# Memory scores in a turn of their own, and V's transposes in another bank, in a hybrid attention layer

## The chip, the cores and the metric

The kernel runs on one core of one Trainium2 chip. The metric is the device time of one execution in microseconds (us); lower is better. The profile is one execution of the same program, taken by the hardware profiler: its engines are PE (TensorE matmuls), PEld (TensorE weight loads), DVE (VectorE), ACT (ScalarE), POOL (GpSimd) and SP (the queue that issues most transfers).

## The reference

One layer of a decoder trunk over 4096 prompt tokens (and 64 sample tokens with caches), width 1024. What matters here is the attention of the prompt:

```python
h = _rmsnorm(x, g_pre); z = h @ w_in
cb, cc, ch, cg, q, k, v, ag, mq, mg = _split_cols(z)
out_a = silu(cg) * cb * conv3(cc * ch)
# window: 8 query heads, 2 kv heads, head_dim 64, blocks of 128 queries
s = q @ k * 0.125 ; s = where(mask, s, -inf)        # 128 own and 128 previous keys
m = maximum(max(s), sink) ; p = exp(s - m)
p = p / (sum(p) + exp(sink - m)) ; o_b = p @ v
# memory: 4 heads, 256 memory tokens
p = softmax(mq @ mk * 0.125) ; o_c = p @ mv
y = concat([out_a, silu(ag) * o_b, silu(mg) * o_c]) @ w_out
x = x + _rmsnorm(y, g_post)
```

## The kernel before, in words

The first part of the program, up to about 931 us, is the input projection (line 368) with its splits and sums; it writes queries, keys, values and gated parts to DRAM. The change does not touch it. The second part interleaves two kinds of work.

**The output projection.** It runs over 33 blocks (`Block.run`, line 1587): 32 of 128 prompt tokens and one of 64 sample tokens. A block's result has two halves of 512 columns (`p`), and each half sums over 8 row tiles (`k`). For one `k` TensorE does three 128x512 matmuls (line 1602), since each operand is split into a high and a low part (`mh`, `ml`, and `wo`). These three matmuls are here called an eighth: a block has 16 eighths.

**The attention.** It runs over half chunks `h = 2c + i` of 128 queries: chunk `c` has 256 tokens, `i` is its half. The half chunks 0 and 1 are done in the first part. The work of each later half chunk is hung into the stream of eighths at places counted from the start of block 0:

- `first_half(h)` at eighth `first_at[h]`: the transposes of the memory probabilities of half `h-1` (tile `xt`, line 1352), the window scores of `h` (`ws`, line 1318), the products of probabilities and values of `h-1` (`wo`, lines 1376, 1382 and 1057), and then, off TensorE, the window softmax of `h` (`sm`) and the gating of `h-1` (lines 1240 and 1393). Where a chunk begins (`i == 0`), V of the chunk is also transposed here (tile `vtp` or `wo`, line 1654), and ScalarE scales the result into `vt` (line 1664).
- `second_half(h)` at eighth `second_at[h]`: the memory scores of `h` (`xs`, line 1340), and right behind them the transposes of the window probabilities (`wt`, line 1364).

Between them the other engines work. For the memory scores: maxima on VectorE (`xmx`, line 1155, and `xnm`), exponentials on ScalarE (`xp`, line 1164), reciprocals on VectorE (`xrd`, line 1170), and the multiplication of `xp` by them on GpSimd (line 1176); only then can `xt` transpose `xp`. For the window: ScalarE copies `wt` to `wpt` (line 1292), GpSimd makes the two masked copies (`wpv`, line 1297, and `wpt`, line 1300), and these go into the products. GpSimd also issues the loads of keys and queries (`kst`, line 1086, and `q`, line 1099). For a block of the projection: `yn` (DVE, line 1609), squares (ACT, line 1610), `yst`, and the split of the next block's input into `mh` (ACT, line 1583) and `ml` (DVE, line 1584).

**PSUM.** All eight banks are given out: two double banks `w` (window scores, window transposes), one double bank `x` (memory scores, memory transposes, products), and two single banks `z` (the projection). The one `x` bank goes round `xt`, `wo`, `xs`: a tile in it can be written once the one before has been read, which for `wo` means the gating, and in a chunk's first half before the change also the scaling of V, which lay in an unused corner of that bank.

**What sets the order.** TensorE's order is the order in which the code is written, up to block 26; after that, and on the other engines throughout, a scheduler puts the instructions in an order when the program is built, and each engine then works strictly in its order.

From half 8 on, `first_at` is one block (16 eighths) after the other, and `second_at` lies 8 eighths behind `first_at`. The halves 2 to 7 are packed more closely by a table of places.

Of the kernel before, what the change touches and what calls it, by code (L numbers as in the profile page):

```python
# [15 lines left out]
P = 128  # L16
# [10 lines left out]
CT = 256  # L27
NCH = 4096 // CT
# [24 lines left out]
def hybrid_layer(ctx: ExitStack, tc: tile.TileContext, a: dict):  # L53
    nc = tc.nc
    TE, V, S, G, DMA = nc.tensor, nc.vector, nc.scalar, nc.gpsimd, nc.sync
# [7 lines left out]
    ident = const.tile([P, P], F32, name="ident")  # L63
# [939 lines left out]
    chunks = {}  # L1003
# [37 lines left out]
    def two_banks(tag, name):  # L1041
        return ps[tag].tile([P, 2, 512], F32, tag=tag, name=name)
# [352 lines left out]
    def chunk_load(c):  # L1395
        if c < NCH:
            chunks[c] = Chunk(c)

            chunks[c].load_queries() if c == 2 else chunks[c].load_keys()
            chunks[c].load_keys() if c == 2 else chunks[c].load_queries()  # L1400
# [238 lines left out]
    def first_half(h):  # L1639

        c, i = divmod(h, 2)
        before = (chunks[(h - 1) // 2], (h - 1) % 2) if 2 < h <= 2 * NCH else None
        if before:
            before[0].memory_transposes(before[1])
        if c < NCH:
            chunks[c].window_scores(i)
        banks = before[0].products(before[1]) if before else None
        new_v = c < NCH and i == 0
        if new_v:
            chunks[c].values(chunks[c - 1].vts[2])  # L1650
            banks = two_banks("x", f"vtp{c}") if banks is None else banks
            t = [banks[:, 1, CT + n * P : CT + n * P + P] for n in range(2)]
            for n in range(2):
                TE.transpose(t[n], chunks[c].vT[:, n * P : n * P + P], ident)
        soon = first_at[h] > 16 * (h - 3) + 4
        if before and soon:
            before[0].gates(before[1], banks)
        if c < NCH:
            chunks[c].window_probabilities(i)
        if before and not soon:  # L1660
            before[0].gates(before[1], banks)
        if new_v:
            for n in range(2):
                S.mul(chunks[c].vts[1 + n], t[n], 0.5)
            chunk_load(c + 1)
        elif c + 1 < NCH:
            chunks[c + 1].load_mix()

    def second_half(h):

        c, i = divmod(h, 2)
        if c < NCH:
            chunks[c].memory_scores(i)
            chunks[c].window_turns(i)


    first_at = {2: 4, 3: 21, 4: 35, 5: 47, 6: 59, 7: 71} | {h: 16 * (h - 3) + 4 for h in range(8, 2 * NCH + 1)}
    second_at = {2: 14, 3: 27, 4: 40, 5: 52, 6: 64, 7: 76} | {h: first_at[h] + 8 for h in range(8, 2 * NCH + 1)}

    def starts_of(i):  # L1680

        at = [(n, lambda h=h: first_half(h)) for h, n in first_at.items()] + [(n, lambda h=h: second_half(h)) for h, n in second_at.items()]
        if i + 1 < len(blocks) and blocks[i + 1].b != 32:
            at.append((max(16 * i, first_at.get(i + 2, 0) + 2), blocks[i + 1].split))
        return {(p, k): lambda now=now: [fn() for fn in now] for p in range(2) for k in range(8)
                if (now := [fn for n, fn in at if n == 16 * i + 8 * p + k])}
# [26 lines left out]
    for i in range(31):  # L1713
        if i == 26:
            turn.close()
        starts = starts_of(i)
        for step in ((p, k) for p in range(2) for k in (1, 3)) if i >= 26 else ():
            starts[step] = lambda before=starts.get(step, lambda: None): (before(), late())
        run(i, starts)
    for stage in stages:  # L1720
        for _ in stage:
            pass
    run(31, starts_of(31))
    run(32, {})
    finish_block()
# [106 lines left out]
```

## Time and profile before

| what | us |
|---|---|
| median of 3 runs | 1549.06 (1541.38 to 1551.43) |
| the profiled execution | 1542.05 |
| its span (first to last instruction) | 1540.3 |
| PE busy in the span | 1520.7 |
| DVE, ACT, POOL busy | 1137.5, 791.0, 393.2 |
| second part (from the first matmul of line 1602) | 931 to 1540 |

Durations and waits below are of the profiled execution. A matmul's duration in the trace is longer than the distance to the next matmul's start, because matmuls are pipelined: what a group costs TensorE is read from its start to the start of the next group.

### The profile page before, as it was taken

What the parts mean: (1) busy time and instruction counts of PE and PEld (TensorE: products, weight loads), DVE (VectorE), ACT (ScalarE), POOL (GpSimd) and SP (SyncE); (2) the same over time, 40 slices, a digit from 0 to 9 for tenths busy, and PEclk for the clock granted to TensorE, in tenths of its full rate; (3) what the DMA queues carried; (4) which work ended last, traced back from release to release, by engine and by line L of the source; (5) the groups of instructions that cost most, each with busy time, mean ns of one, the idle gap of its engine ahead of it and who ended that gap; (6) DMA issues with size and microseconds to landing.
All of it is one profiled execution on the core that took longest, in us unless ns stands there. A gap on an engine that the chain in (4) does not pass through costs nothing.

```text
span 1540.3 us, 30416 instructions
## 1 busy us (share of the span) xinstructions
PE 1520.7 (99%) x11581; PEld 1397.0 (91%) x11581; DVE 1137.5 (74%) x1965; ACT 791.0 (51%) x1949; POOL 393.2 (26%) x635
## 2 busy tenths in 40 slices
PE   9999999999999999999999999999999999999998
PEld 9999999999999999999999998778888888888776
DVE  6789887899988777897677678666666666666653
ACT  6686665476222222445454456555555555555541
POOL 0223232211400000000101203554444444445410
PEclk9999999999999999999999999999999999999999
DMA  9999999878755333678876889967777666666332
GB/s 258 177 240 232 278 284 263 276 241 292 193 180 180 126 126 126 236 223 281 244 269 204 238 295 272 208 140 155 156 155 161 149 149 160 148 148 150 124 123 96
DMA packets 178453, 306.29 MB, mean 199 GB/s; under 512 B 34437, under 2 KB 108165, under 8 KB 178277
## 3 DMA queue, kind: packets, MB, share of 16 engines
q1 hardware_dynamic: 130901, 227.38, 48.2%
q0 software_dynamic: 46688, 75.93, 23.5%
q8 instruction: 91, 1.49, 0.4%
q10 hardware_dynamic: 720, 1.05, 0.2%
q14 instruction: 53, 0.43, 0.1%
HBM read 197.23 MB, written 108.05 MB: 198 GB/s over the span
## 4 chain that ended last, share of the span: by engine, by line
PE 76%; DMA 7%; DVE 5%; POOL 5%; ACT 4%; issue 3%; ACTq 0%; SPq 0%; DVEq 0%; POOLq 0%
PE c L368 47%; PE y L1602 15%; DMA nat<-in_x_p 3%; PE ws L1318 3%; POOL xp L1176 3%; PE wo L1382 2%; PE wo L1057 2%; PE xs L1340 1%; PE wt L1364 1%; PE xt L1352 1%; DMA md<-th 1%; PE wo L1376 1%; POOL wpt L1300 1%; ACT xp L1164 1%; DMA x_0B<-in_xt 1%
## 5 line engine op out<-in xcount | busy, mean ns | idle before, releaser
L1602 PE MATMUL y<-wo,mh 128*128 128x512 f32 (+1 forms) x1040 | 336.1, 394 | 0.0
L375 DVE TENSOR_TENSOR z<-c,z 128x520 f32<-128x520 f32 (+1 forms) x308 | 194.8, 646 | 82.2 <-PE c L368 80.3
L1602 PEld LDWEIGHTS y<-wo,mh 128*128 128x128 f32 x1040 | 194.3, 188 | 42.3 <-issue 4.4
L1602 PE MATMUL y<-wo,ml 128*128 128x512 f32 (+1 forms) x520 | 201.4, 387 | 0.0
L1274 ACT ACTIVATE sm<-sm,wnm 128x128 f32<-128x128 f32 x256 | 99.4, 390 | 70.4 <-DVE wnm L1268 70.4
L1602 PEld LDWEIGHTS y<-wo,ml 128*128 128x128 f32 x520 | 98.0, 188 | 17.7
L1099 POOL DMA_DIRECT2D q<-qd x96 | 59.8, 631 | 139.2 <-PE wt L1364 81.6
L1176 POOL TENSOR_SCALAR xp<-xp,xrd 128x256 f32<-128x256 f32 x128 | 84.9, 675 | 34.8 <-DVE xrd L1170 34.7
L1297 POOL TENSOR_SCALAR_AFFINE_SELECT wpv<-wpt 128x512 f32<-128x512 f32 x62 | 40.4, 665 | 145.4 <-ACT wpt L1292 145.3
L1328 DVE COPY_PREDICATED sm<-wmask,ws 128x512 f32<-128x512 uint8 x60 | 40.6, 732 | 38.2 <-ACT sm L1327 38.2
L737 POOL CAST wmask<-negs 128x256 uint8<-128x256 f32 x1 | 0.9, 930 | 265.8 <-DMA negs<-in_wmask 265.8
L1292 ACT COPY wpt<-wt 128x512 f32<-128x512 f32 x64 | 34.6, 589 | 64.2 <-PE wt L1364 64.2
L1164 ACT ACTIVATE xp<-xs,xnm 128x256 f32<-128x256 f32 x128 | 59.4, 488 | 9.0 <-DVE xnm L1156 6.7
L1155 DVE TENSOR_REDUCE xmx<-xs 128x2 f32<-128x512 f32 x64 | 41.5, 686 | 29.9 <-PE xs L1340 29.8
L1356 ACT COPY xpt<-xt 128x512 f32<-128x512 f32 x30 | 17.6, 586 | 87.3 <-DVE xpt L1356 87.3
L1609 DVE TENSOR_TENSOR yn<-y,gpost 128x512 f32<-128x512 f32 (+1 forms) x66 | 45.1, 683 | 22.1 <-PE y L1602 22.0
L1318 PE MATMUL ws<-kst,q 128*128 128x256 f32 (+1 forms) x480 | 55.8, 298 | 0.0
L276 ACT ACTIVATE nat<-nat 104x1024 f32<-104x1024 f32 x40 | 42.3, 1058 | 26.1 <-DMA nat<-in_x_p 26.1
L1610 ACT ACTIVATE y<-y 128x512 f32<-128x512 f32 (+1 forms) x66 | 39.3, 595 | 30.2 <-DVE yn L1609 30.2
L1300 POOL TENSOR_SCALAR_AFFINE_SELECT wpt<-wpt 128x512 f32<-128x512 f32 x64 | 42.1, 669 | 43.3 <-ACT wpt L1292 43.1
L1356 DVE COPY xpt<-xt 128x512 f32<-128x512 f32 x30 | 20.8, 692 | 42.5 <-PE xt L1352 42.4
L1086 POOL DMA_DIRECT2D kst<-qd x64 | 38.8, 625 | 51.5 <-issue 24.8
(976 smaller groups left out, 5135.5 us busy)
## 6 DMA issues: line engine op xcount, KB each, us to landing
q<-qd POOLq DMA_DIRECT2D x96, 256.0 KB, 4.7
xr<-in_x_p SPq DMA_DIRECT2D x32, 512.0 KB
nat<-in_x_p SPq DMA_DIRECT2D x39, 416.0 KB
o_yp<-xr SPq DMA_DIRECT2D x31, 512.0 KB
md<-th POOLq DMA_DIRECT2D x48, 260.0 KB, 6.6
qd<-zh SPq DMA_DIRECT2D x48, 260.0 KB
qd<-z SPq DMA_DIRECT2D x48, 260.0 KB
kst<-qd POOLq DMA_DIRECT2D x60, 192.0 KB, 4.6
```

Of the source, the lines that this page charges most:

```text
L276: S.activation(t[:RG], t[:RG], AF.Square, accum_out=r[:RG, i : i + 1])
L368: TE.matmul(bank[:, :HW], l, r, start=first and i == 0, stop=last and i == 3 * KH - 1)
L375: add = lambda dst, other: V.tensor_tensor(dst, c, other, op=ALU.add)
L1099: G.dma_start(self.q[64 * half : 64 * half + 64, i : i + 4, :].rearrange("p (j v) n -> p j v n", v=2), heads(part, j, self.ts))
L1155: V.tensor_reduce(mx[:, :nb], s, axis=AX.X, op=ALU.max)
L1164: S.activation(p[:, i, :], s[:, i, :], AF.Exp, bias=nm[:, i : i + 1], scale=SCALE, accum_out=den[:, i : i + 1])
L1176: G.tensor_scalar(p[:, i, :], p[:, i, :], self.rds[h][:, i : i + 1], 0.5, op0=ALU.mult, op1=ALU.mult)
L1274: S.activation(sm[:, hh, :], sm[:, hh, :], AF.Exp, bias=nm[:, hh : hh + 1], scale=SCALE, accum_out=den[:, hh : hh + 1])
L1300: G.affine_select(p3, p3, pattern=[[0, 4], [1, P]], compare_op=ALU.is_ge, fill=0.0, base=0, channel_multiplier=-1)
L1318: TE.matmul(out(kvh, col, bank), q(kvh, col, bank)[r], k(kvh, part)[r], start=first, stop=True, skip_group_check=not first, **place)
L1602: TE.matmul(acc, self.hl[l][:, k], wo[k][c0 // 512][:, r, c0 % 512 : c0 % 512 + c1 - c0], start=j == 0, stop=j == passes * KT - 1)
L1609: V.tensor_tensor(yn[:m, c0:c1], acc[:m], gpost[:m, c0:c1], op=ALU.mult)
```

## The change

The memory scores leave `second_half` and get a turn of their own, `memory_half`, with places `memory_at`. From half 8 on this turn lies 6 eighths behind `first_at`, so two eighths ahead of the window transposes, which stay 8 eighths behind. V's transposes, and the scaling, move from `first_half` into `second_half`, behind the window transposes, and into a double bank `w` in place of the corner of the `x` bank. The table of places for halves 2 to 7 is changed.

```diff
     def first_half(h):
...
         banks = before[0].products(before[1]) if before else None
-        new_v = c < NCH and i == 0
-        if new_v:
-            chunks[c].values(chunks[c - 1].vts[2])
-            banks = two_banks("x", f"vtp{c}") if banks is None else banks
-            t = [banks[:, 1, CT + n * P : CT + n * P + P] for n in range(2)]
-            for n in range(2):
-                TE.transpose(t[n], chunks[c].vT[:, n * P : n * P + P], ident)
...
-        if new_v:
-            for n in range(2):
-                S.mul(chunks[c].vts[1 + n], t[n], 0.5)
+        if c < NCH and i == 0:
             chunk_load(c + 1)
...
-    def second_half(h):
+    def memory_half(h):
         c, i = divmod(h, 2)
         if c < NCH:
             chunks[c].memory_scores(i)
+    def second_half(h):
+        c, i = divmod(h, 2)
+        if c < NCH:
+            if i == 0:
+                chunks[c].values(chunks[c - 1].vts[2])
             chunks[c].window_turns(i)
+            if i == 0:
+                t = two_banks("w", f"vtp{c}")[:, 0].rearrange("p (a n) -> p a n", a=4)
+                for n in range(2):
+                    TE.transpose(t[:, n], chunks[c].vT[:, n * P : n * P + P], ident)
+                for n in range(2):
+                    S.mul(chunks[c].vts[1 + n], t[:, n], 0.5)
...
-    first_at = {2: 4, 3: 21, 4: 35, 5: 47, 6: 59, 7: 71} | {h: 16 * (h - 3) + 4 for h in range(8, 2 * NCH + 1)}
-    second_at = {2: 14, 3: 27, 4: 40, 5: 52, 6: 64, 7: 76} | {h: first_at[h] + 8 for h in range(8, 2 * NCH + 1)}
+    first_at = {2: 4, 3: 19, 4: 33, 5: 46, 6: 59, 7: 71} | {h: 16 * (h - 3) + 4 for h in range(8, 2 * NCH + 1)}
+    memory_at = {2: 11, 3: 24, 4: 38, 5: 51, 6: 64, 7: 76} | {h: first_at[h] + 6 for h in range(8, 2 * NCH + 1)}
+    second_at = {2: 14, 3: 27, 4: 41, 5: 54, 6: 67, 7: 79} | {h: first_at[h] + 8 for h in range(8, 2 * NCH + 1)}
```

On PE, in a chunk's first half in the middle of the second part, the memory scores and the window transposes stand in one turn before the change (`y_1` is the second half of a projection block, `xs_0` the memory scores, `wt` the window transposes; the last number of a name tells tiles of one name apart):

```order
L1602 MATMUL y_1_15509<-wo_1_11845,mh_15162 128x512
L1340 MATMUL xs_0_15522<-mk,q_15055 128x256 x8
L1364 MATMUL wt_15555<-ident,sm_0_15437 128x128 x4
L1364 MATMUL wt_15555<-ident,sm_1_15438 128x128 x4
L1602 MATMUL y_1_15509<-wo_1_11848,mh_15162 128x512
```

At the same place with the change:

```order
L1602 MATMUL y_1_15510<-wo_1_11826,mh_15169 128x512
L1340 MATMUL xs_0_15517<-mk,q_15055 128x256 x8
L1602 MATMUL y_1_15510<-wo_1_11842,mh_15169 128x512
L1602 MATMUL y_1_15510<-wo_1_11842,ml_15170 128x512
...
L1602 MATMUL y_1_15510<-wo_1_11845,mh_15169 128x512
L1364 MATMUL wt_15558<-ident,sm_0_15440 128x128 x4
L1364 MATMUL wt_15558<-ident,sm_1_15441 128x128 x4
L1676 MATMUL vtp_15577<-ident,vT_15053 128x128 x2
L1602 MATMUL y_1_15510<-wo_1_11848,mh_15169 128x512
```

The scores now come six projection matmuls earlier, and V's two transposes (`vtp`) stand behind the window transposes; before, they stood behind the products of the first half.

On POOL, in the same half chunk before the change (`wpv` and `wpt` are the masked copies, `xp` the memory probabilities, `yst` a projection block's norm factor, `kst` the next keys' load):

```order
L1297 AFFINE_SELECT wpv_0_15566<-wpt_0_15564 128x512
L1297 AFFINE_SELECT wpv_1_15571<-wpt_1_15569 128x512
L1300 AFFINE_SELECT wpt_0_15564<-wpt_0_15564 128x512
L1300 AFFINE_SELECT wpt_1_15569<-wpt_1_15569 128x512
L1176 TENSOR_SCALAR xp_0_15539<-xp_0_15539,xrd_0_15547 128x256 x2
L1176 TENSOR_SCALAR xp_1_15543<-xp_1_15543,xrd_1_15551 128x256 x2
L1616 TENSOR_TENSOR yst_15367<-yst_15367,mhalf 128x1
L1086 DMA kst_15915<-qd 64x2x384 x4
```

With the change:

```order
L1176 TENSOR_SCALAR xp_0_15534<-xp_0_15534,xrd_0_15542 128x256 x2
L1176 TENSOR_SCALAR xp_1_15538<-xp_1_15538,xrd_1_15546 128x256 x2
L1297 AFFINE_SELECT wpv_0_15569<-wpt_0_15567 128x512
L1297 AFFINE_SELECT wpv_1_15574<-wpt_1_15572 128x512
L1300 AFFINE_SELECT wpt_0_15567<-wpt_0_15567 128x512
L1300 AFFINE_SELECT wpt_1_15572<-wpt_1_15572 128x512
L1616 TENSOR_TENSOR yst_15374<-yst_15374,mhalf 128x1
L1086 DMA kst_15917<-qd 64x2x384 x4
```

The four multiplications of `xp` have moved from behind the masked copies to ahead of them. In a chunk's second half POOL also issues four loads of `kst` and some of `q` ahead of this; there the two issues of `q` that stood among the masked copies now stand together ahead of `xp`.

On ACT, the same half chunk before the change, behind the last exponential of the window softmax:

```order
L1664 ACTIVATE vt_0_15433<-wo_1_15416 128x128
L1664 ACTIVATE vt_1_15434<-wo_1_15416 128x128
L1610 ACTIVATE y_0_15368,yst_15367<-y_0_15368 128x512
L1292 COPY wpt_0_15564<-wt_15555 128x512
L1292 COPY wpt_1_15569<-wt_15555 128x512
L1164 ACTIVATE xp_0_15539,xden_0_15540<-xs_0_15522,xnm_0_15532 128x256 x2
L1164 ACTIVATE xp_1_15543,xden_1_15544<-xs_0_15522,xnm_1_15536 128x256 x2
L1583 COPY mh_15595<-mix_14834 128x1024
```

With the change:

```order
L1610 ACTIVATE y_0_15375,yst_15374<-y_0_15375 128x512
L1164 ACTIVATE xp_0_15534,xden_0_15535<-xs_0_15517,xnm_0_15527 128x256 x2
L1164 ACTIVATE xp_1_15538,xden_1_15539<-xs_0_15517,xnm_1_15531 128x256 x2
L1292 COPY wpt_0_15567<-wt_15558 128x512
L1292 COPY wpt_1_15572<-wt_15558 128x512
L1678 ACTIVATE vt_0_15556<-vtp_15577 128x128
L1678 ACTIVATE vt_1_15557<-vtp_15577 128x128
L1583 COPY mh_15603<-mix_14840 128x1024
```

The exponentials `xp` have moved ahead of the copies of `wt`, and the two scalings of V from the head of this stretch to behind those copies.

3 lines of the change are left out of this document (2 added, 1 removed).

## The prediction

> **What bounds the kernel now.** I read the page first: the busy times and the chain.
>
> ```profile
> PE 1520.7 (99%) x11581; PEld 1397.0 (91%) x11581; DVE 1137.5 (74%) x1965; ACT 791.0 (51%) x1949; POOL 393.2 (26%) x635
> ...
> PE 76%; DMA 7%; DVE 5%; POOL 5%; ACT 4%; issue 3%; ACTq 0%; SPq 0%; DVEq 0%; POOLq 0%
> ```
>
> TensorE is busy almost throughout, so nothing is gained by making another engine faster; only time in which TensorE waits can be won. A busy TensorE hides short waits, though: a late weight load shows in the next step of a group. So the second view is the waits of the weight loads.
>
> ```profile
> PEld xt L1352 <- POOL xp L1176: 15.8, 45, 1.2
> PEld xs L1340 <- ACT vt L1664: 1.9, 2, 0.9
> ```
>
> The one large wait: the memory transposes `xt` wait for GpSimd's multiplication of `xp`. The other row is the `x` bank held by V's scaling, twice. How much of the 15.8 us costs time is read from the timeline of TensorE, from start to start. First the steady part (a chunk's second half, then the next one's first):
>
> ```profile
> 1102.23 1.11 PE L1340 MATMUL xs<-mk,q 128*128 128x256 f32 x8
> 1103.18 1.04 PE L1364 MATMUL wt<-ident,sm 128*128 128x128 f32 x8
> 1103.98 0.47 PE L1602 MATMUL y<-wo,mh 128*128 128x512 f32 x1
> 1104.29 0.40 PE L1602 MATMUL y<-wo,ml 128*128 128x512 f32 x1
> 1104.53 0.62 PE L1602 MATMUL y<-wo,mh 128*128 128x512 f32 x2
> ...
> 1109.55 1.65 PE L1352 MATMUL xt<-ident,xp 128*128 128x128 f32 x8
> 1110.95 1.86 PE L1318 MATMUL ws<-kst,q 128*128 128x256 f32 x16
> 1112.74 0.43 PE L1376 MATMUL wo<-wpv,vt 64*64 64x256 f32 x2
> ...
> 1115.22 0.44 PE L1654 MATMUL wo<-ident,vT 128*128 128x128 f32 x2
> 1115.42 0.48 PE L1602 MATMUL y<-wo,mh 128*128 128x512 f32 x1
> ...
> 1120.98 1.11 PE L1340 MATMUL xs<-mk,q 128*128 128x256 f32 x8
> ...
> 1128.26 1.29 PE L1352 MATMUL xt<-ident,xp 128*128 128x128 f32 x8
> 1129.31 1.86 PE L1318 MATMUL ws<-kst,q 128*128 128x256 f32 x16
> ```
>
> Eight transposes without a wait take 0.80 us (`wt`: 1103.18 to 1103.98). `xt` takes 1.40 here (1109.55 to 1110.95) and 1.05 in the next half (1128.26 to 1129.31): 0.60 and 0.25 us of waiting, in turn. Reading the 30 groups of `xt` like this, less 0.80 each, gives 13.3 us. The first and the last do not wait, and the largest wait lies in the closely packed halves:
>
> ```profile
> 949.41 1.03 PE L1352 MATMUL xt<-ident,xp 128*128 128x128 f32 x8
> 950.20 1.51 PE L1318 MATMUL ws<-kst,q 128*128 128x256 f32 x10
> ...
> 999.71 0.63 PE L1352 MATMUL xt<-ident,xp 128*128 128x128 f32 x4 [0.82 <-ACT xp L1164]
> 1001.30 0.99 PE L1352 MATMUL xt<-ident,xp 128*128 128x128 f32 x4 [0.96 <-POOL xp L1176]
> 1002.05 1.20 PE L1318 MATMUL ws<-kst,q 128*128 128x256 f32 x8
> ...
> 1485.30 1.06 PE L1352 MATMUL xt<-ident,xp 128*128 128x128 f32 x8
> 1486.12 0.48 PE L1602 MATMUL y<-wo,ml 128*128 128x512 f32 x1
> ```
>
> Of the 13.3 us, 3.6 lie in the first six groups (halves 3 to 8) and 9.7 in the other 24. The same reading of `wt` gives 1.4 us, all in the early halves, and of `xs` 0.3. All that the change can win is thus 15 us, one per cent.
>
> **Why `xt` waits, and what the new order does.** The other engines in the half chunk whose scores stand at 1120.98, and GpSimd and VectorE around 1107:
>
> ```profile
> 1106.61 0.93 POOL L1176 TENSOR_SCALAR xp<-xp,xrd 128x256 f32<-128x256 f32 x2 [0.45 <-DVE xrd L1170]
> 1108.19 1.61 DVE L1584 TENSOR_TENSOR ml<-mix,mh 128x1024 fp32r<-128x1024 f32 x1 [0.40 <-ACT mh L1583]
> 1108.71 1.89 POOL L1176 TENSOR_SCALAR xp<-xp,xrd 128x256 f32<-128x256 f32 x2
> ...
> 1117.97 0.42 DVE L1393 TENSOR_TENSOR mix<-mix,wo 128x256 f32<-128x256 f32 x1
> 1119.15 0.41 ACT L1664 ACTIVATE vt<-wo 128x128 f32<-128x128 f32 x2
> 1120.12 0.69 DVE L1282 TENSOR_TENSOR sm<-sm,wrd 128x512 f32<-128x512 f32 x1
> 1122.12 1.29 DVE L1155 TENSOR_REDUCE xmx<-xs 128x2 f32<-128x512 f32 x2 [1.31 <-PE xs L1340]
> 1123.71 1.23 POOL L1297 TENSOR_SCALAR_AFFINE_SELECT wpv<-wpt 128x512 f32<-128x512 f32 x2 [9.53 <-ACT wpt L1292]
> 1124.89 1.22 POOL L1300 TENSOR_SCALAR_AFFINE_SELECT wpt<-wpt 128x512 f32<-128x512 f32 x2
> 1125.36 0.50 ACT L1164 ACTIVATE xp<-xs,xnm 128x256 f32<-128x256 f32 x1
> 1125.81 1.08 ACT L1583 CAST mh<-mix 128x1024 fp32r<-128x1024 f32 x1
> 1126.10 2.85 POOL L1176 TENSOR_SCALAR xp<-xp,xrd 128x256 f32<-128x256 f32 x4
> 1126.34 0.15 DVE L1170 RECIPROCAL xrd<-xden 128x2 f32<-128x2 f32 x1
> 1129.59 0.69 DVE L1356 COPY xpt<-xt 128x512 f32<-128x512 f32 x1 [1.31 <-PE xt L1352]
> ```
>
> Two things make `xp` late. GpSimd does the four masked copies first (1123.71 to 1126.10). And two multiplications take 0.93 us alone but 1.89 us where `ml` runs on VectorE.
>
> With the change the scores start 18 matmuls behind the products instead of 24 plus V's transposes. From the rows, 24 take 5.56 us (1115.42 to 1120.98) and six take 1.36 (at 0.227 each), so they start at 1115.22 + 4.2 = 1119.4, and their result is there 1.14 us later, as in the row at 1122.12. VectorE is then still at its last window share, until 1120.81. So the chain of maxima, exponentials and reciprocals begins at 1120.8 instead of 1122.1: 1.3 us won. The last exponential, which began at 1125.36, begins at 1124.05; nothing stands in front of it on ScalarE but the squares of `y`. The second reciprocal, at 1126.34 behind VectorE's `yn`, now stands ahead of `yn`, at about 1124.7. GpSimd has no masked copy in front and `ml` comes later, so the second pair ends at 1124.8 + 0.93, near 1125.7 (1126.7 if it meets a stretching row). The `xt` turn is near 1128.4: the wait goes with 1.7 to 2.7 us to spare. In the chunk's other half the odd loads stand ahead of `xp`: two issues of `q`, some 0.6 us each, released when the scores have been read. They end before the first reciprocal and cost nothing.
>
> What is late next? The masked copies now come last: 2.45 us from 1125.7 to 1126.7 on, so they end by 1129.2; the products follow `xt` and `ws`, at 1128.4 + 0.80 + 1.79 = 1131.0. The cover is 1.8 us; if they meet `ml` and are stretched by 1 us, as `xp` was, 0.8. On ScalarE the copies of `wt` wait 1.3 us behind the exponentials and V's scaling (0.8 us) stands ahead of `mh`, so `mh` starts at about 1126.4 instead of 1125.81, and `ml` and `yst` follow 0.6 us later, still ahead of VectorE's copy of `xt` at 1129.59. The cover there is gone at one more microsecond. The `x` bank, needed at 1119.4, is free at 1118.39: cover 1.0 us. The loads of V and of the gated parts on SP move by one place among loads that are needed a block later. V's transposes cost 0.2 us wherever they stand.
>
> **What it adds.** One more change of group per half chunk: scores, then projection, then transposes. A run of projection matmuls starts slowly: 1103.98, 1104.29, 1104.53 are distances of 0.31 and 0.24 against 0.227, so 0.10 us, and over a run of 24 (1103.98 to 1109.55, 5.57 against 5.44) 0.13. Scores followed directly by the projection occur in no row; eight scores take 0.95 us where 16 of `ws` take 1.79, which leaves 0.05 for leaving the group. Bounds: 0, if the extra switch hides, and 0.26, two slow starts. I take 0.15, near the measured start: 30 x 0.15 = 4.5 us (0 to 7.8).
>
> The Trainium skill, "TensorE: Matmul & The Clock Gate", section "The mechanism", says that TensorE pulls a weight load ahead of running matmuls through a 64-deep window, if it goes to other rows or to the background buffer. By that rule a new group would start without a gap and the added term would be 0, not 4.5. The slow starts above speak against it at a change of group.
>
> **Early halves.** There the scores stand 5 eighths behind the first half, as they mostly did, but the next first half follows one eighth (0.68 us) later for halves 2 to 5, and at the same distance for 6 and 7. The 1.54 us wait at 999.71 cannot all go. Of 3.6 + 1.4 us I take half, 2.5 (bounds 0 and 5).
>
> **Sum.** 9.7 + 2.5 - 4.5 = 7.7 us won; with the bounds, from 2 to 15. Against the profiled execution, 1542.05 - 7.7 = 1534.3. The median of the runs shown lies 7.0 us above that execution, though, which no row explains; against the median it is 1541.4. I put the time between, at 1538, and so about 0.5% faster, less than the 1% which a measurement of this kernel can surely tell from no change.
>
> **The rivals.**
>
> *The extra switch is free, or the early waits all go (0.12).* Then 12 to 15 us are won: 1527 to 1530 against the profiled execution, 1534 to 1537 against the median. For it: weight loads do run beside matmuls in all long groups. Against: every run of projection matmuls starts slowly.
>
> *The wait moves to the products (0.16).* The masked copies become GpSimd's last work, and `wo` waits where `xt` did. It decides once they end 0.8 to 1.8 us later than worked out; at 0.3 us a half it takes 30 x 0.3 = 9 us back, and the time is that of before, 1542 to 1549. For it: the closely packed halves have 3 eighths less between `wt` and the products than the steady ones. Against: the steady cover.
>
> *The scores wait for the bank, slower (0.12).* TensorE works strictly in order, so scores that wait for the gating hold up the projection behind them.
>
> ```profile
> 1133.58 0.50 PE L1602 MATMUL y<-wo,mh 128*128 128x512 f32 x1
> 1136.23 0.41 DVE L1393 TENSOR_TENSOR place<-place,wo 128x256 f32<-128x256 f32 x1
> ```
>
> In the other half the gating ends at 1136.64, and the scores come at 1133.58 + 4.2 = 1137.8: cover 1.1. Where VectorE's chain from `xt` to the gating is later by more than 1.0 to 1.1 us, because `ml` and `yst` now follow `mh` later, each further 0.1 us costs 0.1 x 24 = 2.4 us. It eats the gain at 1.4 us late; at 1.8 late it costs 18 - 8 = 10 us net: 1552 against the profiled execution. Beyond 2 us late it is slower by over 1%. Against: the 0.6 us worked out for `ml`.
>
> *The change doesn't do what it says (0.05).* GpSimd's `xp` still meets a long VectorE row and stays late; then only the switches remain: 1542 + 4.5, up to 1554 against the median.
>
> **How the numbers follow.** The forecast, 4 to 11 us won, has 0.55; its own range is 1531 to 1546 over both bases. The range 1530 to 1549 leaves out the lowest part of the first rival and the upper part of the two slow ones, some 0.2. Faster by over 1% is most of the first rival on the lower base and the edge of the forecast: 0.12. Slower by over 1% needs the late bank or the stretched `xp`: 0.08. Within 1%: 0.80.
>
> **What would show it.** Right: the row of `xt` waiting for `xp` falls from 15.8 us to under 4; `xt` groups of 0.80 us from 1060 on; GpSimd's `xp` ahead of the masked copies and in pairs of 0.93; runs of 18, 6 and 24 projection matmuls, each about 0.13 longer than 0.227 a piece. Wrong: `xs` waiting for line 1393, `wo` waiting for lines 1297 or 1300, or six projection matmuls between scores and transposes taking more than 1.6 us. The sum itself would be wrong if the time between two executions of one program moves more than the gain, as the runs of before do.

## The result, and the profile after

| what | before | after |
|---|---|---|
| median of the runs made together, us | 1547.24 (6 runs, 1541.38 to 1551.43) | 1532.99 (6 runs, 1529.56 to 1534.86) |
| the profiled execution, us | 1542.05 | 1534.86 |
| its span, us | 1540.3 | 1532.8 |
| second part, from the first matmul of line 1602 to the end, us | 609.3 | 597.1 |

The ratio of after to before is 0.9909, with a 95% interval of 0.9883 to 0.9935: 0.9% faster, 14 us by the medians. The profiled executions stand only 7.2 us apart, because the first part of the program, which the change does not touch, took 4.8 us longer in the profiled run of after (935.7 us) than in that of before (931.0). Over the 14 profiles of this case it takes 928.3 to 935.7 us without a pattern. So from here on the second part is compared by itself: it became 12.3 us shorter (12.25 before rounding).

The page of after, busy times and chain:

```profile
PE 1517.8 (99%) x11581; PEld 1400.9 (91%) x11581; DVE 1136.7 (74%) x1965; ACT 793.6 (52%) x1949; POOL 389.1 (25%) x635
...
PE 82%; DMA 7%; DVE 6%; issue 2%; ACT 1%; POOL 1%; SPq 0%; DVEq 0%; POOLq 0%; ACTq 0%
```

GpSimd falls from 5% of the chain to 1%, TensorE rises from 76% to 82%. The waits of TensorE's weight loads after the change (what waits, for what: us in total, times, longest):

```profile
PEld y L1602 <- issue: 6.8, 34, 0.4
PEld xt L1352 <- POOL xp L1176: 2.5, 5, 1.2
```

The row of 15.8 us in 45 waits is now 2.5 us in 5. The first row is waits at the starts of the projection's runs. It has grown, but not by the extra turn. Before:

```profile
PEld y L1602 <- issue: 4.4, 20, 0.4
PEld wo L1654 <- issue: 2.4, 14, 0.2
```

The second of these rows belongs to V's transposes. After the change it is gone, and the first row has grown by the same 2.4 us and 14 times. In the runs below that row is 4.4 us in 20 with the turn alone and 6.8 us in 34 with V's move alone, so it grew with V's move. What the turn costs has to be read from start to start. TensorE's timeline in a chunk's first half, the counterpart of the stretch from 1115.42 to 1131.10 before:

```profile
1114.39 0.50 PE L1602 MATMUL y<-wo,mh 128*128 128x512 f32 x1
...
1118.60 1.11 PE L1340 MATMUL xs<-mk,q 128*128 128x256 f32 x8
1119.54 0.39 PE L1602 MATMUL y<-wo,mh 128*128 128x512 f32 x1
1119.77 0.40 PE L1602 MATMUL y<-wo,ml 128*128 128x512 f32 x1
...
1120.93 1.03 PE L1364 MATMUL wt<-ident,sm 128*128 128x128 f32 x8
1121.80 0.38 PE L1676 MATMUL vtp<-ident,vT 128*128 128x128 f32 x2
1121.94 0.48 PE L1602 MATMUL y<-wo,mh 128*128 128x512 f32 x1
1122.25 0.40 PE L1602 MATMUL y<-wo,ml 128*128 128x512 f32 x1
...
1127.52 1.04 PE L1352 MATMUL xt<-ident,xp 128*128 128x128 f32 x8
1128.31 1.86 PE L1318 MATMUL ws<-kst,q 128*128 128x256 f32 x16
1130.09 0.43 PE L1376 MATMUL wo<-wpv,vt 64*64 64x256 f32 x2
```

`xt` takes 0.79 us from start to start (1127.52 to 1128.31): no wait. The same holds in every half from 9 to 28. The six projection matmuls behind the scores take 1.39 us (1119.54 to 1120.93), that is 6 x 0.227 and 0.03; they start evenly, 0.23 apart. The 18 behind the products take 4.21 (1114.39 to 1118.60), 0.13 over 18 x 0.227, and the run behind V's transposes begins with a distance of 0.31 (1121.94 to 1122.25). A slow start costs 0.13 us behind products and transposes and 0.03 behind the scores.

The other engines in the same half, in order of time:

```profile
1117.04 0.41 DVE L1393 TENSOR_TENSOR mix<-mix,wo 128x256 f32<-128x256 f32 x1
1119.79 1.28 DVE L1155 TENSOR_REDUCE xmx<-xs 128x2 f32<-128x512 f32 x2
1122.59 1.91 POOL L1176 TENSOR_SCALAR xp<-xp,xrd 128x256 f32<-128x256 f32 x4 [9.69 <-DVE xrd L1170]
1124.45 1.23 POOL L1297 TENSOR_SCALAR_AFFINE_SELECT wpv<-wpt 128x512 f32<-128x512 f32 x2
1125.63 2.21 POOL L1300 TENSOR_SCALAR_AFFINE_SELECT wpt<-wpt 128x512 f32<-128x512 f32 x2
1125.85 1.50 DVE L1584 TENSOR_TENSOR ml<-mix,mh 128x1024 fp32r<-128x1024 f32 x1 [0.16 <-ACT mh L1583]
```

`xp` ends at 1124.50, 3.0 us ahead of `xt`; the masked copies end at 1127.84, 2.25 ahead of the products; the gating ends at 1117.45, 1.15 ahead of the scores. What meets `ml` now is not `xp` but the last two masked copies. The groups of GpSimd over the 19 steady halves say it in one number each (busy us, mean ns); before:

```profile
L1176 POOL TENSOR_SCALAR xp<-xp,xrd 128x256 f32<-128x256 f32 x77 | 55.3, 728 | 4.5 <-DVE xrd L1170 4.5
L1300 POOL TENSOR_SCALAR_AFFINE_SELECT wpt<-wpt 128x512 f32<-128x512 f32 x37 | 23.0, 632 | 0.0
```

and after:

```profile
L1300 POOL TENSOR_SCALAR_AFFINE_SELECT wpt<-wpt 128x512 f32<-128x512 f32 x39 | 43.7, 1142 | 0.0
L1176 POOL TENSOR_SCALAR xp<-xp,xrd 128x256 f32<-128x256 f32 x76 | 35.4, 478 | 101.6 <-DVE xrd L1170 101.3
```

The stretch of some 20 us did not go; it moved from an operation that TensorE waited for to one with 2 us of cover. The waits that are left lie in the closely packed halves 6 and 7:

```profile
1002.72 0.60 PE L1352 MATMUL xt<-ident,xp 128*128 128x128 f32 x4
1003.63 1.00 PE L1352 MATMUL xt<-ident,xp 128*128 128x128 f32 x4 [0.31 <-POOL xp L1176]
1004.39 1.86 PE L1318 MATMUL ws<-kst,q 128*128 128x256 f32 x16
...
1019.42 0.60 PE L1352 MATMUL xt<-ident,xp 128*128 128x128 f32 x4
1020.95 1.00 PE L1352 MATMUL xt<-ident,xp 128*128 128x128 f32 x4 [0.93 <-POOL xp L1176]
1021.71 1.86 PE L1318 MATMUL ws<-kst,q 128*128 128x256 f32 x16
```

These two groups take 1.67 and 2.29 us, 0.88 and 1.50 over the 0.79.

### The profile page after: what moved, and what is told of

Same layout as the page of the kernel before. It is cut to its first block, busy times and chain, and to the rows that moved or that the text cites. A ratio compares the mean times of both kernels' runs of the same rounds, so it can differ in the third digit from the quotient of the medians.

```text
span 1532.8 us, 30521 instructions
## 1 busy us (share of the span) xinstructions
PE 1517.8 (99%) x11581; PEld 1400.9 (91%) x11581; DVE 1136.7 (74%) x1965; ACT 793.6 (52%) x1949; POOL 389.1 (25%) x635
## 3 DMA queue, kind: packets, MB, share of 16 engines
q8 instruction: 92, 1.51, 0.4%
## 4 chain that ended last, share of the span: by engine, by line
PE 82%; DMA 7%; DVE 6%; issue 2%; ACT 1%; POOL 1%; SPq 0%; DVEq 0%; POOLq 0%; ACTq 0%
PE c L368 43%; PE y L1602 23%; DMA md<-th 3%; PE ws L1318 3%; PE wo L1382 2%; PE wo L1057 2%; PE xs L1340 2%; PE xt L1352 2%; PE wt L1364 2%; PE wo L1376 1%; DMA nat<-in_x_p 1%; DVE z L375 1%; PE mem_acc L789 1%; DMA place<-in_xt 1%; DMA ws10A<-in_w_in 1%
## 5 line engine op out<-in xcount | busy, mean ns | idle before, releaser
L1602 PE MATMUL y<-wo,mh 128*128 128x512 f32 (+1 forms) x1040 | 341.7, 394 | 0.0
L1176 POOL TENSOR_SCALAR xp<-xp,xrd 128x256 f32<-128x256 f32 x128 | 61.5, 492 | 173.8 <-DVE xrd L1170 173.3
L1300 POOL TENSOR_SCALAR_AFFINE_SELECT wpt<-wpt 128x512 f32<-128x512 f32 x64 | 63.3, 1008 | 43.4 <-ACT wpt L1292 43.1
L407 ACT CAST zh<-z 128x520 fp32r<-128x520 f32 x56 | 33.3, 624 | 36.1 <-DVE z L375 31.9
L1318 PEld LDWEIGHTS ws<-kst,q 128*128 128x128 f32 (+1 forms) x480 | 46.5, 187 | 4.1
L377 ACT COPY z<-c 128x520 f32<-128x520 f32 (+1 forms) x44 | 24.4, 554 | 48.6 <-PE c L368 45.5
L1274 ACT ACTIVATION_READ_ACCUMULATOR sm<-sm,wnm 128x1 f32 x256 | 47.8, 187 | 0.0
```

What stands on the lines that cost most here:

```text
L1176: G.tensor_scalar(p[:, i, :], p[:, i, :], self.rds[h][:, i : i + 1], 0.5, op0=ALU.mult, op1=ALU.mult)
L1274: S.activation(sm[:, hh, :], sm[:, hh, :], AF.Exp, bias=nm[:, hh : hh + 1], scale=SCALE, accum_out=den[:, hh : hh + 1])
L1300: G.affine_select(p3, p3, pattern=[[0, 4], [1, P]], compare_op=ALU.is_ge, fill=0.0, base=0, channel_multiplier=-1)
L1318: TE.matmul(out(kvh, col, bank), q(kvh, col, bank)[r], k(kvh, part)[r], start=first, stop=True, skip_group_check=not first, **place)
L1602: TE.matmul(acc, self.hl[l][:, k], wo[k][c0 // 512][:, r, c0 % 512 : c0 % 512 + c1 - c0], start=j == 0, stop=j == passes * KT - 1)
```

## The experiments

Each kernel is read in three stretches of its second part. They are bounded by starts in TensorE's timeline: **early** from the first matmul of line 1602 to the `xt` group of half 9, **steady** from there to that of half 28 (19 halves), **tail** from there to the end.

| kernel | early | steady | tail | second part |
|---|---|---|---|---|
| before | 123.4 | 351.1 | 134.8 | 609.3 |
| the change | 119.5 | 343.4 | 134.2 | 597.1 |
| the change, a second profile | 119.8 | 343.4 | 134.1 | 597.4 |
| the turn from half 8 on, alone | 124.4 | 343.7 | 134.6 | 602.7 |
| V's move alone | 124.2 | 348.5 | 134.9 | 607.7 |
| turn and V, old table | 125.6 | 343.4 | 134.2 | 603.2 |
| GpSimd's order alone | 122.6 | 371.2 | 139.9 | 633.7 |
| the change, turn at +4 | 119.6 | 350.9 | 135.8 | 606.3 |
| the change, turn at +7 | 119.4 | 342.7 | 134.6 | 596.6 |
| turn and table, V as before | 118.7 | 343.6 | 134.6 | 596.9 |
| before, `wt` ahead of `xs` | 126.5 | 342.0 | 134.7 | 603.3 |
| the combination | 118.6 | 342.0 | 134.7 | 595.4 |

The second profile of the change differs by 0.3 us from the first, so half a microsecond in this table is readable, where times of whole runs tell 0.2% apart at best (3 us). Each stretch is rounded by itself, so a row can miss its sum by 0.1.

**The turn alone.** The old table; the scores leave the common turn from half 8 on; V as before.

```diff
     def second_half(h):
...
-            chunks[c].memory_scores(i)
+            if h not in memory_at:
+                chunks[c].memory_scores(i)
             chunks[c].window_turns(i)
+    # memory_half(h) as in the change
+    memory_at = {h: first_at[h] + 6 for h in range(8, 2 * NCH + 1)}
```

The halves 2 to 7 stay as before.

> The kernel before, with the memory scores in a turn of their own from half 8 on (6 eighths behind the first half); V's transposes stay in the x bank, the old table of places stays. The second part (first matmul of line 1602 to the end) took 609.3 us before and 597.1 with the change. Theory (GpSimd order and lead cure xt, but the bank is then held by V's scaling): xt waits of the 24 steady halves fall from 9.7 to under 1 us, but xs waits for the scaling of V by 0.3 to 0.6 us in each of 12 chunks, 4 to 7 us in all; second part 603 to 607. Rival (V's bank does not matter): no waits of xs, second part 599 to 601.

Measured: 0.9929 of before (0.9902 to 0.9956). Waits of the weight loads:

```profile
PEld xt L1352 <- POOL xp L1176: 5.7, 10, 1.2
PEld xs L1340 <- ACT vt L1664: 4.6, 14, 0.9
```

The steady stretch is the change's to 0.3 us: there the turn is the whole gain, and all waits of `xt` that are left are early ones. The scores now meet V's scaling in the bank they share, 14 times, but most of it is a weight load's wait that runs beside matmuls: read from the groups it costs some 0.09 us each, less than was expected. The second part, 602.7, lies between the two ranges.

**V's move alone.**

```diff
-    # V's transposes and scaling in first_half, in the x bank
+    # V's transposes and scaling in second_half, behind window_turns, in a w bank
```

> The changed kernel with the memory scores back in one turn with the window transposes and with the old table of places; only V's transposes are moved (behind the window transposes, into a w bank). Theory (V's bank alone leaves the lateness of xp): xt waits in the steady halves stay at 8 to 10 us, the early waits of xs for V's scaling (1.3 us) go, second part 606 to 608. Rival (the bank was what the change cured): second part below 602.

Measured: 0.9983 (0.9968 to 0.9999). Waits:

```profile
PEld xt L1352 <- POOL xp L1176: 12.0, 32, 1.2
...
PE wt L1364 <- DVE sm L1282: 2.7, 4, 1.0
```

The second part, 607.7, is as the theory had it, the waits are not: from half 9 on those of `xt` fall from 9.7 to 6.7 us, where 8 to 10 were expected. V's move cures `xt` in one half of a chunk, where the wait was 0.25, and leaves the 0.6 of the other. In the early halves `wt` now waits for its shares. 1.6 us in all: little.

**Turn and V with the old table.** What differs from the change is the table of places for halves 2 to 7 and, with it, the separate turn in these halves.

```diff
-    first_at = {2: 4, 3: 19, 4: 33, 5: 46, 6: 59, 7: 71} | ...
-    memory_at = {2: 11, 3: 24, 4: 38, 5: 51, 6: 64, 7: 76} | ...
-    second_at = {2: 14, 3: 27, 4: 41, 5: 54, 6: 67, 7: 79} | ...
+    first_at = {2: 4, 3: 21, 4: 35, 5: 47, 6: 59, 7: 71} | ...
+    second_at = {2: 14, 3: 27, 4: 40, 5: 52, 6: 64, 7: 76} | ...
+    # memory_at from half 8 on only; in halves 2 to 7 the scores in second_half, as before
```

> The changed kernel with the old table of places for halves 2 to 7, where the scores then stand in one turn with the window transposes as before; from half 8 on as in the change. Theory (the table is worth a small part): steady halves without waits of xt, early waits 2 to 3 us more than with the change; second part 599 to 600.5. Rival (the table is worth nothing): 597 to 597.5. Rival (most of the gain is the table's): over 603.

Measured: 0.9940 (0.9919 to 0.9961). The steady stretch is the change's; the early one is 6.1 us longer, more than was expected of the table: the second part, 603.2, is in the second rival's range. Part of the 6.1 is that the turn from half 8 on and V's move cost 2.1 us in the early stretch with the old table (125.6 against 123.4 of before). What the new table would be worth without a separate turn in the early halves was not tried.

**GpSimd's order alone.** Before, with `xp` and the masked copies kept on GpSimd in the order in which they are written, so `xp` ahead of the copies, and the scores no earlier.

```diff
-                G.tensor_scalar(p[:, i, :], p[:, i, :], self.rds[h][:, i : i + 1], 0.5, op0=ALU.mult, op1=ALU.mult)
+                x = G.tensor_scalar(p[:, i, :], p[:, i, :], self.rds[h][:, i : i + 1], 0.5, op0=ALU.mult, op1=ALU.mult)
+                if self.c:
+                    tc.keep_in_program_order(x)
...
+    # the same for the two masked copies, lines 1297 and 1300
```

> The kernel before with one thing changed: GpSimd's order, in which the four multiplications of xp are put ahead of the masked copies; scores, V and table stand where they stood. Theory G (GpSimd's order is most of it): with 0.47 us a piece and no copies ahead, xp ends at or just before the turn of xt; steady waits of xt fall from 9.7 to under 3 us, second part 600 to 603. Theory L (the lead of two eighths is what does it): they stay above 6 us, second part over 605. If the masked copies then come too late, it shows as waits of line 1376.

Measured: 1.0138 (1.0112 to 1.0165), slower. Here six lines were added, so `xt` is line 1358, the first products 1382 and the masked copies 1299 and 1304:

```profile
PEld wo L1382 <- POOL wpt L1304: 26.6, 26, 1.6
...
PEld xt L1358 <- POOL xp L1176: 3.5, 14, 0.5
...
PE wo L1382 <- POOL wpt L1304: 13.9, 14, 1.1
```

GpSimd in one of these halves:

```profile
1111.16 2.00 POOL L1176 TENSOR_SCALAR xp<-xp,xrd 128x256 f32<-128x256 f32 x2
1113.13 0.62 POOL L1299 TENSOR_SCALAR_AFFINE_SELECT wpv<-wpt 128x512 f32<-128x512 f32 x1
...
1116.72 0.65 POOL L1304 TENSOR_SCALAR_AFFINE_SELECT wpt<-wpt 128x512 f32<-128x512 f32 x1
```

`xp` is still stretched, and the last copy ends at 1117.37, while the products had started at 1115.31; they stop until 1117.42. From half 9 on the waits of `xt` fall to 1.5 us, as theory G had it, but the time doesn't follow. The wait of `xt` has become a larger wait of the products: the rival of the prediction, made to happen. So the order on GpSimd is worth something only with scores that come early enough.

**The change once more**, as a measure of what two profiles of one program differ by.

> The changed kernel itself, timed beside the others of this call. Its second part took 597.1 us in the first profile, 343.4 of them in the steady stretch (first memory transposes of half 9 to those of half 28), 119.5 ahead of it. Expected again within 0.5 us, while the first part may differ by some us; ratio of the times to the kernel before 0.990 to 0.994.

Measured: 0.9927 (0.9910 to 0.9944); the second part 597.4.

**Half chunks at an even distance of 15 eighths** until they join the 16 of the later ones.

```diff
-    first_at = {2: 4, 3: 19, 4: 33, 5: 46, 6: 59, 7: 71} | {h: 16 * (h - 3) + 4 for h in range(8, 2 * NCH + 1)}
...
+    first_at = {h: 4 + max(15 * (h - 2), 16 * (h - 3)) for h in range(2, 2 * NCH + 1)}
+    memory_at = {h: n + 6 for h, n in first_at.items()}
+    second_at = {h: n + 8 for h, n in first_at.items()}
```

> The changed kernel with another table: half h begins at eighth 4 + 15(h-2) until this meets 16(h-3), so the halves 2 to 18 are spaced evenly by 15 eighths in place of 12 to 15 for 2 to 7 and then 16; the scores are always 6, the window transposes always 8 eighths behind. Theory (the waits left are those of the close packing): the 4 us of waits that the change still has in halves 2 to 8 go; second part 592.5 to 594.5, time 0.2 to 0.3% below the changed kernel. Rival (they come from the start of the second part, whatever the spacing, or turn up later): 596 us or more.

Measured: 0.9966 (0.9949 to 0.9982), slower than the change (0.9927); the second part 602.3. Halves 3 to 7 have no waits, as the early theory said, but new ones come elsewhere:

```profile
PE wo L1376 <- ACT xpt L1356: 3.6, 2, 2.4
PE wt L1364 <- DMA qd<-z: 1.3, 1, 1.3
```

The rival's side. The first row is the products in halves 15 and 16; `xt` also waits in halves 8, 10 and 13, by 0.6 to 1.3 us. The second row is at the very start, in half 2, whose window transposes come two eighths earlier here and, by the row, wait for a transfer. At this distance the half chunks slide by one eighth a time against the blocks of the projection and their own work (`yn`, `mh`, `ml`); that this phase is what makes the later ones wait is likely, but was not tried by itself. (Its `xt` group of half 9 comes at another eighth, so it has no line in the table.)

**The turn two eighths earlier, and one later.**

```diff
-    memory_at = {...} | {h: first_at[h] + 6 for h in range(8, 2 * NCH + 1)}
+    memory_at = {...} | {h: first_at[h] + 4 for h in range(8, 2 * NCH + 1)}   # one kernel
+    memory_at = {...} | {h: first_at[h] + 7 for h in range(8, 2 * NCH + 1)}   # the other
```

> The changed kernel with the scores four eighths behind the first half from half 8 on, not six. In the profile of the change the gating ends 1.15 us ahead of the scores' turn, and two eighths are 1.36 us; on VectorE the maxima of the scores now also stand between the two window shares. Theory (one bank goes round): scores wait for line 1393 by about 0.2 us a half, and the window transposes for the delayed share by 0.2 to 0.6; steady stretch of 19 halves 351 to 358 us, against 343.4. Rival (an earlier turn is free): 343 to 345.

> The changed kernel with the scores seven eighths behind the first half, one ahead of the window transposes. In the profile of the change xp is ready 3.0 us ahead of the turn of xt; one eighth is 0.68. Theory (GpSimd's order, which is the same here, did most, and the lead has room): no waits of xt, steady stretch 343 to 344.5 us. Rival (the lead of two eighths is needed in full): xt waits 0.2 us or more a half, steady stretch over 347.

Measured, +4: 1536.39 us in its one run, the steady stretch 350.9, 7.5 us longer than the change's and at the low edge of what was expected.

```profile
PEld xs L1340 <- PE y L1602: 13.2, 23, 0.7
```

In one half, VectorE and TensorE:

```profile
1111.01 0.41 DVE L1393 TENSOR_TENSOR mix<-mix,wo 128x256 f32<-128x256 f32 x1
1111.52 1.18 PE L1340 MATMUL xs<-mk,q 128*128 128x256 f32 x8 [0.15 <-PE y L1602]
```

The scores start at 1111.52, 0.10 us behind the end of the gating at 1111.42; from half 8 on it is 0.10 or 0.15 us in every half, against some 1.1 with the change. So they wait for the `x` bank, 0.4 us a half (7.5 over 19), and hold up the projection behind them, though the rows name `y` as what came last. That is the prediction's slow rival, at a place where the lead is 1.4 us larger. The other wait that was expected, of the window transposes for a late share, doesn't come. Measured, +7: 1532.40 us in its one run, steady 342.7, a little under the range expected, and no wait of `xt` from half 9 to half 28. The lead has at least 0.7 us of room on the side of `xt`.

**Turn and new table, with V as before.**

```diff
-    # V's transposes in second_half, in a w bank
+    # V's transposes in first_half, in the x bank, as before
```

> The change without its part on V: separate turn and new table, V's transposes behind the products in the x bank as before. Theory (V's bank matters only where the scores come early after the products): steady stretch 343.5 to 344.5 us (343.4 with the change), early stretch 120 to 121.5 (119.5 to 119.8 with the change), second part 597.5 to 599.5. Rival (V's move is what lets the new table work): early stretch over 122.5, second part over 600.5.

Measured: 0.9925 (0.9910 to 0.9940); the second part 596.9, the change's to 0.2 us. The scores meet V's scaling again:

```profile
PEld xs L1340 <- ACT vt L1664: 4.6, 14, 0.7
...
PE xs L1340 <- ACT vt L1664: 0.6, 3, 0.3
```

but 0.6 us of idle time is all of it that TensorE shows. With the turn and the table in place, moving V brings nothing: it saves some 0.1 us in the steady stretch and 0.5 in the tail, and costs 0.7 early. The 1.50 us wait of `xt` that the change keeps in half 7 is V's: with V as before this group takes 0.79 us.

**Half chunks at 16 eighths from the start**, so that there is no packed stretch.

```diff
-    first_at = {2: 4, 3: 19, 4: 33, 5: 46, 6: 59, 7: 71} | {h: 16 * (h - 3) + 4 for h in range(8, 2 * NCH + 1)}
...
+    first_at = {h: 16 * (h - 2) + 4 for h in range(2, 2 * NCH + 1)}
+    memory_at = {h: n + (7 if h == 2 else 6) for h, n in first_at.items()}
+    second_at = {h: n + (10 if h == 2 else 8) for h, n in first_at.items()}
```

> The changed kernel with every half one full block behind the one before, from half 2 on, so that the whole attention keeps the place in a block that the steady halves have and ends one block later. Theory (the waits left in the change come from the places of the packed halves in a block): no waits of xt, wo or wt but the first, 4 us less; at the end two more halves stand beside the sample tokens' work, which may cost up to 3; second part 593 to 596 against 597.1. Rival (the crowded end gives it back): 597 to 602.

Measured: 0.9953 (0.9936 to 0.9970); the second part 601.0. All early waits of `xt` are gone, and the end, where the last half chunk now meets the sample tokens' attention, takes more than that back:

```profile
PE sms L1445 <- DMA sq<-in_cmk: 3.7, 3, 2.2
```

The rival again (and, as above, no line in the table). The close packing of the early halves buys room at the end.

**Before, with the local transposes ahead of the memory scores** in their common turn: one pair of lines exchanged, no turn of its own.

```diff
     def second_half(h):
...
-            chunks[c].memory_scores(i)
             chunks[c].window_turns(i)
+            chunks[c].memory_scores(i)
```

> The kernel before with the window transposes ahead of the memory scores in their one turn, so that the projection follows the scores and not the transposes. Theory (the slow start of a run of projection matmuls belongs to the group ahead of it): runs behind the scores take 0.03 us over 0.227 a piece, not 0.13, in this kernel too, 0.10 won per half; but the scores come 0.8 us later, so xt waits 0.5 to 1.2 us a half and the second part is 611 to 622 against 609.3. Rival (each turn costs its 0.13 whatever is in it): no run under 0.10.

Measured: 1536.44 us in its one run, the second part 603.3. The first part of the theory holds: projection runs behind the scores lose 0.02 us at their start. What was expected of `xt` in the steady halves was wrong: the scores come 0.8 us later than before, and yet `xt` waits nowhere in the steady halves. The stretch, 342.0, is 1.4 us shorter than the change's. The reason stands in the timeline of one half, TensorE, GpSimd and VectorE together:

```profile
1122.65 1.03 PE L1364 MATMUL wt<-ident,sm 128*128 128x128 f32 x8
1123.44 1.17 PE L1340 MATMUL xs<-mk,q 128*128 128x256 f32 x8
1124.44 1.23 POOL L1297 TENSOR_SCALAR_AFFINE_SELECT wpv<-wpt 128x512 f32<-128x512 f32 x2 [8.95 <-ACT wpt L1292]
...
1125.61 1.23 POOL L1300 TENSOR_SCALAR_AFFINE_SELECT wpt<-wpt 128x512 f32<-128x512 f32 x2
1127.72 1.85 POOL L1176 TENSOR_SCALAR xp<-xp,xrd 128x256 f32<-128x256 f32 x4 [0.88 <-DVE xrd L1170]
1129.30 1.34 DVE L1584 TENSOR_TENSOR ml<-mix,mh 128x1024 fp32r<-128x1024 f32 x1 [0.77 <-ACT mh L1583]
1129.91 1.03 PE L1352 MATMUL xt<-ident,xp 128*128 128x128 f32 x8
```

`wt` is ready 0.9 us earlier, so GpSimd has done its copies (to 1126.84) before the first reciprocal is there, and the exponentials ahead of `mh` put `ml` later, to 1129.30. None of the eight GpSimd operations is stretched, and `xp` ends at 1129.57, just ahead of `xt` at 1129.91. The last `xp` is still running when `ml` begins, in every steady half, but it keeps its 0.47 us: here it is `ml` that takes longer, 1.34 and 1.58 us in turn. In the other half of a chunk `xp` ends just as `xt` starts. So there is no room left; it is enough that each `xp` begins ahead of `ml`, or within 0.05 us of its start. What made `xt` wait before was less that the copies stood ahead of `xp` than that they started late and pushed `xp` into `ml`. The early stretch is worse, 126.5: with the old table `wt` waits there for the shares of the window.

**The combination.** Turn, new table for halves 2 to 7 and V as before; from half 8 on the exchange in place of the separate turn.

```diff
     def second_half(h):
...
             chunks[c].window_turns(i)
+            if h not in memory_at:
+                chunks[c].memory_scores(i)
...
-    memory_at = {2: 11, 3: 24, 4: 38, 5: 51, 6: 64, 7: 76} | {h: first_at[h] + 6 for h in range(8, 2 * NCH + 1)}
+    memory_at = {2: 11, 3: 24, 4: 38, 5: 51, 6: 64, 7: 76}
```

> The change's first eighths and its separate turn of the scores for halves 2 to 7, V's transposes in the x bank, and from half 8 on no separate turn: the local transposes first and the memory scores right behind them, in one turn eight eighths after the first. Theory, from the run with the exchange alone: in the steady halves it is enough that the memory scores and the local transposes change places, because GpSimd then has its masked copies done before the shares are there, and the copies as well as xp end before the DVE subtraction ml begins; one slow start a half goes too. So the stretch from half 9 to half 28 takes 342.0 us, the early one 118.7 to 119.5, the tail 134.7: the second part takes 595 to 596 us, 1 to 2 us less than the change's 597.1, with xp in pairs of 0.93 us and no idle time of the memory transposes from half 9 on. In time that is about 0.1% below the change, 1531 to 1533 us: not to be told from it by time, only by the trace. Rival: the exchange ran well only because its early part was late by 7 us against the loads and stores; with the early part on time the score groups of a steady half come 0.8 us too late again, xp's last slice (0.1 us ahead of its transposes there) is waited for with 0.2 to 0.5 us a half, and the second part takes 599 to 605 us, 1534 to 1541 us in time.

Measured: 1530.25 us median (1528.61 to 1532.83), 0.9915 of before (0.9901 to 0.9929). The second part takes 595.4, as the theory had it: early 118.6, steady 342.0, tail 134.7. One thing that it excluded came: in half 30, in the tail, `xt` takes 1.51 us, 0.7 of it waiting (the same in the run with the exchange alone). GpSimd over the steady halves:

```profile
L1176 POOL TENSOR_SCALAR xp<-xp,xrd 128x256 f32<-128x256 f32 x76 | 35.1, 475 | 7.9 <-DVE xrd L1170 7.9
L1300 POOL TENSOR_SCALAR_AFFINE_SELECT wpt<-wpt 128x512 f32<-128x512 f32 x38 | 24.2, 650 | 0.0
```

Neither group is stretched now (728 and 632 ns before, 478 and 1142 with the change). Against the change TensorE's runs of projection cost 2.6 us less in the 19 halves, one slow start of 0.13 less each, and the scores 1.4 more, 1.02 us a group instead of 0.945 where they follow transposes. With the rest, 0.2 less, that is the 1.4 by which the stretch is shorter. The whole is 1.7 us shorter than the change by the traces; by the times the two can't be told apart.

## Why the prediction was right, and where it was not

The change makes the kernel faster by less than 1%, as forecast, but by more than the 7.7 us worked out: 12.3 us in the second part, 14 by the medians, and so outside the 4 to 11 us won that had 0.55. The measured 1533.0 lies 5 us under the predicted 1538. That the profiled run, 1534.86, stands beside the 1534.3 worked out against the profile is luck: its first part took 4.8 us longer. Point by point:

- **The wait of `xt`, 9.7 us from half 9 on.** Right. In the steady halves the `xt` groups take 15.0 us instead of 23.5, in the tail 4.0 instead of 5.4: 9.9 us won. The turn alone gives all of the steady part.
- **Why it goes.** Right in this kernel: `xp` stands ahead of the copies, in pairs of 0.93 (1.91 for four), and ends before `ml`. The covers were 3.0 us for `xp` (1.7 to 2.7 worked out), 2.25 for the copies (1.8; 0.8 if stretched, and they are stretched, 2.21 us for the pair) and 1.15 for the `x` bank (1.0 to 1.1). But the exchange of the two groups shows that the lead wasn't needed, only that the last `xp` begins no later than `ml`; the first of the two reasons given for a late `xp`, the copies in front, was not enough by itself.
- **The extra turn, 4.5 us.** Wrong, the first term mis-sized. "Scores followed directly by the projection occur in no row", and the value taken was that of a start behind transposes. Measured is 0.03 us behind scores, and 0.8 us over 19 halves for all of the projection. With what V's move adds and takes, the 24 halves from 9 on paid 1.6 us (9.9 won of `xt` less 8.3 won in all) where 24 x 0.15 = 3.6 was put. And 0.6 of this 1.6 lies in the tail, in two groups of the sample tokens' attention (`sms` 2.58 to 3.01 us, `swt` 0.91 to 1.08). The Trainium skill, "TensorE: Matmul & The Clock Gate", section "The mechanism", from which a term of 0 followed, was nearer here than the rows that were set against it; behind products and transposes the start of 0.13 stays, which that rule does not give.
- **The early halves, 2.5 us.** Too low, the second term mis-sized: with the six switches put at 0.9, 1.6 net was expected and 4.0 came. Half of the waits was a guess; 4.2 us stay, 2.4 of them in the groups of `xt` shown above. And there was more to win than the 15 us counted: idle time of 0.97 and 0.9 us ahead of the first matmul of `xt` in halves 6 and 7 (the row at 999.71 has 0.82 of it) belongs, from start to start, to the projection's run before it, and was left out. It went. So did 1.3 us that the projection's runs ahead of `xs` lost to V's scaling in halves 4 and 6, 0.66 each; of that wait only the 0.3 inside the groups of `xs` had been counted.
- **The rivals.** The time came out as in the first one, the switch nearly free and most of the early waits gone (12 to 15 us won), which had 0.12: of the two terms that it names, both moved its way. The wait at the products exists, at 0.2 to 0.3 us in three packed halves, and becomes the whole story where GpSimd's order is changed without the lead. The scores' wait for the bank comes at +4, not at +6. The change did what it says.
- **The three parts.** The prediction did not divide them. The turn is worth all of the steady gain (351.1 to 343.7), the table with the turn the early one, V's move nothing in all (597.1 against 596.9).

The two mis-sized terms account for the difference: 9.9 for 9.7, 1.6 paid for 3.6, and 4.0 for 1.6 make 12.3 for 7.7.

## What to carry to other kernels

When an off-path engine makes TensorE wait, look at what lengthens its operation as much as at what stands in front of it: here two orders, one with `xp` first and one with the copies first, both cure the wait, because in each the last `xp` begins before a long VectorE row with two inputs, or with it. A second look at the order of two neighbouring groups is cheaper than a turn of its own. And an engine that is 99% busy by its page can still have 2% of a stretch to win (12.3 of the 609.3 us here): read distances from start to start, and count the idle time ahead of a group's first instruction too.

## What the runs showed of the hardware that was not expected

- A run of 128x512 projection matmuls starts with a loss of about 0.13 us (0.10 to 0.15 in the steady halves before and with the change) behind 128x128 transposes and behind the products, and of 0.02 to 0.03 behind the scores (1.39 us for six with the change, 5.465 for 24 in the combination, at 0.2267 each). Scores that follow transposes take 1.02 us, and 0.945 behind projection. Why was not tried.
- `ml` on VectorE, with two inputs in SBUF, and GpSimd's `xp` and masked copies take turns. In the steady halves of before, the change, the exchange and the combination, a GpSimd operation that is under way when `ml` begins, or begins within 0.05 us, keeps its 0.47 or 0.63 us; `ml` then ends 1.07 to 1.14 us behind the last such one, and takes up to 1.75 us instead of 1.23. One that begins later ends about 0.34 (`xp`) or 0.49 us (a copy) behind the end of `ml`, and so takes up to 1.49 us before and 1.67 with the change. The Trainium skill, "SBUF — State Buffer", section "Who interferes with whom", says that a VectorE instruction with two SBUF inputs contends with a GpSimd instruction that reads SBUF; these rows agree, and add the price: up to one microsecond for a GpSimd operation that comes second, 0.1 to 0.5 us for `ml` where it does.
- The untouched first part varies by 7 us between executions of programs that are alike in it. What it hangs on stayed open; it is half of what the change wins, and a comparison of two whole profiled spans would have given 7.5 us for 12.3.
